# Moving most transfers of a two-block float32 network from the SyncE queue to the GpSimd queue, and its reciprocal square roots from GpSimd to VectorE

## The chip, the cores and the metric

The kernel runs on one core of a Trainium2 chip. The metric is the device time of one execution in microseconds (us). Engine names are those of the profile: PE is TensorE (PEld its weight loads), DVE is VectorE, ACT is ScalarE, POOL is GpSimd, SP is SyncE; a trailing q (SPq) means the engine's own instruction queue, where transfers are issued.

## What is computed

One sequence of 256 rows and 2048 features, float32, goes through two layers of a first block and one layer of a second. Cut to what matters here:

```
c_act = silu(c)
for l in range(2):
    mod = c_act @ w_mod[l] + b_mod[l]            # 2048 -> 3 * 2048
    shift, scale, gate = split(mod, 3)
    h = rmsnorm(x, norm_gain[l]) * (1 + scale) + shift
    proj = h @ w_in[l]                           # q_a k_a v_a g_a q_i k_i w_i q_b k_b v_b g_b
    y_a = sparse_attention(rmsnorm(q_a), rmsnorm(k_a), v_a, q_i, k_i, w_i, rel_bias) * silu(g_a)
    y_b = head_groupnorm(retention(rotary(q_b), rotary(k_b), v_b)) * silu(g_b)
    x = x + gate * (concat(y_a, y_b) @ w_out[l])
...
u = rmsnorm(x) @ w_in_2          # then a gated convolution, a gated recurrence with its own rmsnorm
x = x + (...) @ w_o_2
x = x + sigmoid(rmsnorm(x) @ w_ple_gate_2) * (p @ w_ple_proj_2)
return rmsnorm(x)
```

Every norm ends in (sum * mean + eps) ** -0.5 of a column of 1, 2 or 4 numbers per partition.

## The kernel before

**Tiles.** The 256 rows are two tiles of 128 (t = 0, 1). A weight is read in chunks of two row blocks by 512 columns (128 x 2 x 512, 512 KB). `wchunk` (L221) loads a chunk into `raw` (three buffers), ACT casts it to float32r (`whi`, L231) and DVE subtracts to get the rest (`wlo`, L233). `wgroup` (L236) then issues twelve matmuls per chunk (L249 to L251: three products, two row blocks, two row tiles).

**Modulation.** `gemv` (L333) computes the product of one row with `w_mod`, beside the matmuls and off PE: 16 transfers of 512 KB into `graw` (three buffers, L347), each followed by one DVE instruction that multiplies and accumulates (`acc`, L351 for the first, L353 for the others). One gemv of 16 gives a quarter of a layer's shift and scale (`mod_quarter`, L356, which ends in `Gm`, L366) or half of its gate (`mod_gate`, L376). There are 12 gemvs, 192 transfers. The very first one (layer 0, quarter 0, `wide`) takes six of its loads through `raw` buffers.

**Order.** Background jobs (gemvs, the bias table, selection, attention, retention) are Python generators that are stepped once per weight chunk at the rates of a table. The order that results on each engine's queue is then set by a scheduler at build time. At run time every engine works through its own list strictly in order, and so does every queue that issues transfers.

**The first ten projections of layer 0** run in four passes (`per = 4`, L834), each over a quarter of the features; a pass needs the rows scaled with that quarter's `Gm`. `bias_table` (L439) runs beside passes 1 to 3: 12 times it loads `rb` (L457), makes one-hot rows on ACT (L462 to L465), multiplies on PE (L469), copies `bt` on ACT (L471) and stores it (L472).

**The end of a layer.** `out_proj` (L874) loads the old rows (`xo`, L885), adds, stores to `xd` (L890), and at its last columns calls `drain()` (L893), which puts every background job still open ahead of what follows. Then `row_rstd` (L201: `tot`, L203, and `rstd`) gives the scale of the next layer's rows (ACT, L912).

**Issue.** SP issues all transfers but a few at the start: 512 KB weight chunks (L226), `graw` (L347), `rb`, `bt` stores, attention's `L` (L675), retention's `dec` (L756), `xo`, `xd` and the final stores. POOL issues 16 small loads at the start (L300, L308, L443).

**rstd** (L149) runs on POOL: six instructions, of which one is a power (L154). It is called 33 times.

Of the kernel before, what the change touches and what calls it, by code (L numbers as in the profile page):

```python
# [27 lines left out]
# steps of each background job per weight chunk  # L28
# [3 lines left out]
# places that instructions move forward in the order of issue  # L32
# [7 lines left out]
def shape_constants():  # L40
    """Tables that depend on shapes alone."""
# [27 lines left out]
def build(tc, a, out):  # L69
# [4 lines left out]
    with es:  # L74
# [5 lines left out]
        # ---------------------------------------------------------------- helpers  # L80
# [20 lines left out]
        def step(n=1):  # L101
            """Advance every background job by its rate."""
# [12 lines left out]
        def spawn(gen, rate, then=None):  # L115
            """Start a background job; another may follow it."""
            bg.append([gen, rate, 0.0, then])
# [10 lines left out]
        def give(consumer, t, pt):  # L128
            """Run a consumer up to its yield; what follows waits for flush()."""
            r = consumer(t, pt)  # L130
            if r is not None:
                next(r)
                late.append(r)
# [15 lines left out]
        def rstd(ss, n, mean):  # L149
            """(ss * mean + EPS) ** -0.5 for a [P, n] tile of sums of squares."""  # L150
            v = sm(n, "rv")
            G.tensor_scalar(v, ss, mean, EPS, op0=OP.mult, op1=OP.add)  # L152
            y = sm(n, "ry")
            G.tensor_tensor(y, v, mhalf[:, 0:n], op=OP.pow)  # L154
            q = sm(n, "rq")
            G.tensor_mul(q, y, y)
            G.tensor_mul(q, q, v)
            G.tensor_scalar(q, q, -0.5, 1.5, op0=OP.mult, op1=OP.add)
            z = sm(n, "rz")
            G.tensor_mul(z, y, q)  # L160
            return z
# [6 lines left out]
        def split_ps(ps, gain=None):  # L168
            """A [P, 512] transposed block in PSUM into its two float32r parts."""
# [36 lines left out]
        def build_kg(src, kg, gains, shifts):  # L206
            """One tile of four transposed blocks: normed rows scaled, shifted, split."""
# [9 lines left out]
        def build_raw(src, kg, gains):  # L217
            """Four transposed blocks of rows that are still to be normed, times the norm's gains."""
            return split_ps(transpose4(src), gains[:, kg * 4:kg * 4 + 4])

        def wchunk(srcs, n, kt):  # L221
            """Two row blocks of a weight, loaded and split."""
# [13 lines left out]
        def wgroup(srcs, n, aT, kts, consumer, mode="k", tw=3):  # L236
            """out[t] = rows[t] @ W for one group of columns; kts are row blocks (pairs from even)."""
# [41 lines left out]
        # ---------------------------------------------------------------- constants, small vectors  # L279
# [9 lines left out]
        mhalf = con.tile([P, 4], F32, name="mhalf")  # L289
        G.memset(mhalf, -0.5)  # L290
# [35 lines left out]
        # ---------------------------------------------------------------- modulation  # L326
# [6 lines left out]
        def gemv(l, ranges, wide=False):  # L333
            acc = b1.tile([P, 1024], F32, name="acc", tag="acc", bufs=2)
            for j in range(16):
# [10 lines left out]
                with tc.high_priority(offset=AHEAD["gdma"]):  # L346
                    last[1] = Y.dma_start(dst, src)  # L347
# [28 lines left out]
        def mod_gate(l, q):  # L376
            """Half q of layer l's gate, on every partition."""
            for acc in gemv(l, [4096 + 1024 * q, 4096 + 1024 * q + 512]):
                yield
            for i in range(2):  # L380
                c0 = 1024 * q + 512 * i
                gb = ev()
                Y.dma_start(gb, a["b_mod"][l, 4096 + c0:4096 + c0 + 512][None, :].to_broadcast([P, 512]))
# [10 lines left out]
        # ---------------------------------------------------------------- T5 bias table, rotary tables  # L394
# [8 lines left out]
        def rel_rotary(ap):  # L403
# [9 lines left out]
            for t in range(2):  # L413
# [4 lines left out]
                Y.dma_start(reld[t], rb[:, 0:(t + 1) * P])  # L418
# [20 lines left out]
        def bias_table(ap):  # L439
# [13 lines left out]
            for t, r0 in jobs:  # L453
# [3 lines left out]
                Y.dma_start(rb, bass.AP(tensor=reld[t].tensor, offset=reld[t].offset + r0 * ns,  # L457
                                        ap=[[32 * ns, 4], [0, 32], [1, nr * ns]]))
                h2 = nr // 2
                for hf in range(2):  # L460
# [11 lines left out]
                    Y.dma_start(bass.AP(tensor=biasd[t].tensor,  # L472
# [4 lines left out]
        # ---------------------------------------------------------------- start  # L477
# [75 lines left out]
        # ---------------------------------------------------------------- block 1  # L553
        def from_ps(pt, sb):
            """Columns in SBUF: as they are, or copied out of PSUM."""
# [6 lines left out]
        def layer(l, hT, ap):  # L562
# [62 lines left out]
            def select(t):  # L625
                """0 where a key is among the TOPK of its row and not after it, NEG elsewhere."""
# [726 lines left out]
```

## Time and profile before

| | |
|---|---|
| three runs | 1963.08, 1964.33, 1960.91 us; median 1963.08 |
| profiled execution, first to last instruction | 1964.1 us, 1.0 us above that median |
| PE busy | 1849.0 us, 94% |
| DVE busy | 1313.3 us, 67% |
| ACT busy | 1044.1 us, 53% |
| POOL busy | 93.0 us, 5% |
| moved by transfers | 440.37 MB, mean 224 GB/s |

The time of the profiled execution is its span; the page gives no other time for it, so the span is what later sums start from. The busy shares are averages over stages with different limits, so a stage is read by itself: PE's idle time in it, what the DMA engines moved in it, and which wait ended last.

### The profile page before, as it was taken

The page shows a single profiled execution, that of the slowest core. Times are in us where ns is not written, and L with a number is a line of the kernel's source. Part 1 is how long each engine was busy: PE and PEld are TensorE (multiplying, and loading weights), DVE is VectorE, ACT ScalarE, POOL GpSimd, SP SyncE. Part 2 cuts the span into 40 slices and gives each one's busy share as a digit, 9 for nine tenths or more (in the row PEclk, how much of TensorE's full clock was granted, in tenths as well). Part 3 has the DMA queues.
Part 4 walks back from the last instruction along what each step waited for, and adds up shares of the span by engine and source line. Part 5 has one row for each costly group of instructions (what it writes and reads, how often), then busy time and mean ns, then how long its engine had stood idle before and what let it go on. Part 6 is the DMA issues. An engine that isn't in the chain of part 4 may idle for free.

```text
span 1964.1 us, 24148 instructions
## 1 busy us (share of the span) xinstructions
PE 1849.0 (94%) x8670; PEld 1503.6 (77%) x8670; DVE 1313.3 (67%) x1713; ACT 1044.1 (53%) x1576; POOL 93.0 (5%) x220
## 2 busy tenths in 40 slices
PE   3988899998997999999999999999999999999997
PEld 3866577777776877688878878888888888888786
DVE  6787669998777677976755565656575545455554
ACT  3557484554435455447545675458445444445554
POOL 2000011001101002100000100000000000000100
PEclk9999899999998999999999999999999999999999
DMA  9987777987888898875547765556656666657564
GB/s 316 327 269 251 249 234 224 320 293 235 295 300 264 295 309 282 269 223 157 163 156 239 214 181 174 151 171 183 177 151 191 194 193 193 193 183 222 176 205 146
DMA packets 230921, 440.37 MB, mean 224 GB/s; under 512 B 19728, under 2 KB 32144, under 8 KB 230672
## 3 DMA queue, kind: packets, MB, share of 16 engines
q1 hardware_dynamic: 228880, 436.38, 70.5%
q10 hardware_dynamic: 1440, 2.34, 0.3%
q8 instruction: 68, 1.11, 0.2%
q14 instruction: 53, 0.43, 0.1%
q0 software_dynamic: 480, 0.10, 0.0%
HBM read 430.85 MB, written 7.91 MB: 223 GB/s over the span
## 4 chain that ended last, share of the span: by engine, by line
PE 60%; DMA 15%; DVE 11%; ACT 5%; issue 5%; POOL 3%; SPq 1%; ACTq 0%; DVEq 0%; POOLq 0%
PE mm L250 18%; PE mm L251 18%; PE mm L249 18%; DMA graw<-in_w_mod_dram 8%; DVE wlo L233 5%; DMA raw<-in_w_in_dram 4%; DMA rb<-reld 2%; ACT whi L231 2%; DVE acc L353 2%; PE tr L196 2%; PE tr L1070 1%; POOL ry L154 1%; DVE I L648 1%; POOL rv L152 1%; SPq L226 1%
## 5 line engine op out<-in xcount | busy, mean ns | idle before, releaser
L233 DVE TENSOR_TENSOR wlo<-raw,whi 128x1024 fp32r<-128x1024 f32 (+1 forms) x596 | 721.6, 1213 | 409.5 <-ACT whi L231 407.8
L231 ACT CAST whi<-raw 128x1024 fp32r<-128x1024 f32 (+1 forms) x596 | 621.9, 1045 | 696.7 <-PE mm L251 451.3
L250 PE MATMUL mm<-wlo,ah 128*128 128x512 f32 (+1 forms) x2368 | 935.8, 395 | 23.5 <-DVE wlo L233 23.2
L249 PE MATMUL mm<-whi,ah 128*128 128x512 f32 (+1 forms) x2368 | 934.5, 397 | 11.8 <-ACT ah L187 7.7
L251 PE MATMUL mm<-whi,al 128*128 128x512 f32 (+1 forms) x2368 | 931.0, 393 | 0.7 <-DVE al L188 0.6
L250 PEld LDWEIGHTS mm<-wlo,ah 128*128 128x128 f32 x2368 | 449.0, 190 | 132.2 <-DVE wlo L233 44.6
L249 PEld LDWEIGHTS mm<-whi,ah 128*128 128x128 f32 x2368 | 447.7, 189 | 108.8 <-ACT ah L187 8.4
L251 PEld LDWEIGHTS mm<-whi,al 128*128 128x128 f32 x2368 | 448.5, 189 | 92.1 <-DVE al L188 2.2
L353 DVE SCALAR_TENSOR_TENSOR acc<-graw,ct,acc 128x1024 f32<-128x1024 f32 x174 | 223.0, 1282 | 63.4 <-DMA graw<-in_w_mod_dram 62.8
L851 DVE TENSOR_TENSOR sp<-sp,mm 128x512 f32<-128x512 f32 (+1 forms) x64 | 42.0, 660 | 15.1 <-PE mm L251 15.0
L196 PE MATMUL tr<-blob,ev 128*128 128x128 f32 x192 | 34.2, 277 | 5.2 <-DVE ev L737 4.1
L179 ACT ACTIVATE ev<-tr,vT 128x128 f32<-128x128 f32 x112 | 32.4, 378 | 9.9 <-PE tr L196 9.3
L481 ACT ACTIVATE junk<-xs 128x512 bf16<-128x512 f32 (+1 forms) x42 | 25.6, 610 | 21.5 <-DMA xs<-in_x_dram 9.4
L152 POOL TENSOR_SCALAR rv<-tot 128x1 f32<-128x1 f32 (+1 forms) x9 | 3.7, 413 | 652.9 <-DVE tot L203 639.6
L154 POOL TENSOR_TENSOR ry<-rv,mhalf 128x4 f32<-128x4 f32 (+2 forms) x33 | 34.2, 1036 | 2.8
L196 PEld LDWEIGHTS tr<-blob,ev 128*128 128x128 f32 x192 | 23.6, 140 | 13.5 <-issue 6.0
L196 PE MATMUL tr<-blob,xs 128*128 128x128 f32 x128 | 24.5, 285 | 8.8 <-ACT xs L912 6.3
L462 ACT ACTIVATE oh<-rb,blob 128x512 f32<-128x512 uint8 x24 | 16.2, 715 | 27.0 <-DMA rb<-reld 27.0
L1070 PEld LDWEIGHTS tr<-X 128*128 128x128 f32 x224 | 27.0, 192 | 2.0 <-ACT uT L1119 1.0
L1070 PE MATMUL tr<-X 128*128 128x128 f32 x224 | 27.5, 276 | 0.1
L196 PEld LDWEIGHTS tr<-blob,xs 128*128 128x128 f32 x128 | 16.8, 146 | 13.8 <-ACT xs L912 7.4
L469 PE MATMUL ms<-ohr,rb 128*32 128x512 f32 x48 | 16.0, 428 | 11.2 <-ACT ohr L465 11.1
(275 smaller groups left out, 1183.8 us busy)
## 6 DMA issues: line engine op xcount, KB each, us to landing
raw<-in_w_in_dram SPq DMA_DIRECT2D x416, 512.0 KB
graw<-in_w_mod_dram SPq DMA_DIRECT2D x186, 512.0 KB
raw<-in_w_out_dram SPq DMA_DIRECT2D x64, 512.0 KB
raw<-in_w_o_dram SPq DMA_DIRECT2D x32, 512.0 KB
raw<-in_w_ple_gate_dram SPq DMA_DIRECT2D x32, 512.0 KB
raw<-in_w_a_out_dram SPq DMA_DIRECT2D x16, 512.0 KB
raw<-in_w_b_out_dram SPq DMA_DIRECT2D x16, 512.0 KB
raw<-in_w_in_dram SPq DMA_DIRECT2D x16, 256.0 KB
```

Source lines behind the costliest of these rows:

```text
L154: G.tensor_tensor(y, v, mhalf[:, 0:n], op=OP.pow)
L179: A.activation(e[:, s], ps[:, s], AF.Copy, scale=gain[:, i:i + 1])
L196: T.transpose(ps[:, s], src[:, s], ident)
L231: A.copy(hi, raw)
L233: V.tensor_sub(lo, raw, hi.bitcast(F32))
L249: T.matmul(o, ah, hi[:, j, :], start=first, stop=False)
L250: T.matmul(o, ah, lo[:, j, :], start=False, stop=False)
L251: T.matmul(o, al, hi[:, j, :], start=False, stop=end)
L353: last[0] = V.scalar_tensor_tensor(acc, rf, ct[:, j:j + 1], acc, op0=OP.mult, op1=OP.add)
L481: A.activation(junk[:, :n], src, AF.Square, accum_out=acc)
L851: V.tensor_add(h, h, pt[:, :n])
L1070: T.matmul(ps[:, h * P:(h + 1) * P], X[:, h, s], X[:, h, s], start=True, stop=True)
```

## The change

**Queues.** `gemv` loads (but for those of the first gemv), the gate's bias loads, `reld`, `rb` and bias-table stores, `L`, `dec`, `xo`, `xd` and the second block's `xo` are issued by POOL. SP keeps the weight chunks, the first gemv, the two loads of positions, and single loads and stores of the second block. **rstd** runs on DVE: an integer guess from the bits of the argument and three Newton steps, twelve dependent instructions where POOL had six.

```diff
         def rstd(ss, n, mean):
             v = sm(n, "rv")
-            G.tensor_scalar(v, ss, mean, EPS, op0=OP.mult, op1=OP.add)
+            V.tensor_scalar(v, ss, mean, EPS, op0=OP.mult, op1=OP.add)
             y = sm(n, "ry")
-            G.tensor_tensor(y, v, mhalf[:, 0:n], op=OP.pow)
-            q = sm(n, "rq")
-            G.tensor_mul(q, y, y)
-            G.tensor_mul(q, q, v)
-            G.tensor_scalar(q, q, -0.5, 1.5, op0=OP.mult, op1=OP.add)
-            z = sm(n, "rz")
-            G.tensor_mul(z, y, q)
-            return z
+            V.tensor_scalar(y.bitcast(I32), v.bitcast(I32), 1, None, op0=OP.logical_shift_right)
+            V.tensor_scalar(y.bitcast(I32), y.bitcast(I32), -1.0, 1597463007.0, op0=OP.mult, op1=OP.add)
+            for _ in range(3):
+                q = sm(n, "rq")
+                V.scalar_tensor_tensor(q, y, -0.5, y, op0=OP.mult, op1=OP.mult)
+                V.tensor_mul(q, q, v)
+                z = sm(n, "rz")
+                V.scalar_tensor_tensor(z, q, 1.5, y, op0=OP.add, op1=OP.mult)
+                y = z
+            return y
...
-                    last[1] = Y.dma_start(dst, src)
+                    last[1] = (Y if wide else G).dma_start(dst, src)
...
-                Y.dma_start(rb, bass.AP(tensor=reld[t].tensor, offset=reld[t].offset + r0 * ns,
+                G.dma_start(rb, bass.AP(tensor=reld[t].tensor, offset=reld[t].offset + r0 * ns,
...
-                    Y.dma_start(bass.AP(tensor=biasd[t].tensor,
+                    G.dma_start(bass.AP(tensor=biasd[t].tensor,
...
-                    Y.dma_start(L, biasd[t][hs].rearrange("h t s -> t h s"))
+                    G.dma_start(L, biasd[t][hs].rearrange("h t s -> t h s"))
-                    Y.dma_start(dec, a["k_dec"][:, 4 * g + h, :])
+                    G.dma_start(dec, a["k_dec"][:, 4 * g + h, :])
...
-                    Y.dma_start(xo, src[t * P:(t + 1) * P, j * 512:(j + 1) * 512])
+                    G.dma_start(xo, src[t * P:(t + 1) * P, j * 512:(j + 1) * 512])
-                    Y.dma_start(xd[t * P:(t + 1) * P, j * 512:(j + 1) * 512], n)
+                    G.dma_start(xd[t * P:(t + 1) * P, j * 512:(j + 1) * 512], n)
...
```

Comments and docstrings are dropped, so lines move by up to three. The scheduler makes a new order from the new queues. Three places show it; the names are those of the program, and `x4` is four alike in a row.

On SP, in the second pass of layer 0 (bias-table stores at L472, `rb` loads at L457), the order before was:

```order
L226 DMA raw<-in_w_in_dram 128x2x512 x2
L347 DMA graw<-in_w_mod_dram 128x2x512
L472 DMA biasd_84<-bt 4x8x512
L226 DMA raw<-in_w_in_dram 128x2x512
L472 DMA biasd_84<-bt 4x8x512
L347 DMA graw<-in_w_mod_dram 128x2x512
L457 DMA rb<-reld_86 128x1x1024
```

and over the passes of layer 0 it is now:

```order
L229 DMA raw<-in_w_in_dram 128x2x512 x3
L406 DMA pti<-in_positions_dram 128x2x1
L409 DMA tmp<-in_positions_dram 128x256
L229 DMA raw<-in_w_in_dram 128x2x512
L229 DMA raw<-in_w_in_dram 128x2x80
L229 DMA raw<-in_w_in_dram 128x2x256
L229 DMA raw<-in_w_in_dram 128x2x80
L229 DMA raw<-in_w_in_dram 128x2x256
L229 DMA raw<-in_w_in_dram 128x2x512 x18
```

Nothing stands between weight chunks on SP any more; the store that waits for `bt` stands on POOL, between `graw` loads.

On DVE, at the end of the first gemv, where the first scaled rows are made (`Sh` and `Gm` scale them, `ev` and `al` are the rows), the order before was:

```order
L353 SCALAR_TENSOR_TENSOR acc<-graw,ct,acc 128x1024 x4
L412 MEMSET hp 128x1
L441 MEMSET rbd 128x32
L314 COPY vT<-ms 128x128
L315 COPY vT_75<-ms 128x64
L363 TENSOR_TENSOR Sh_79<-tr,vT 128x4
L365 TENSOR_TENSOR mq<-tr,vT 128x4
L316 SCALAR_TENSOR_TENSOR gqk<-vT_75 128x2
L366 SCALAR_TENSOR_TENSOR Gm_77<-mq,vT 128x4
```

and is now, from that `vT` on:

```order
L315 COPY vT<-ms 128x128
L352 TENSOR_SCALAR acc<-graw,ct 128x1024
L316 COPY vT_73<-ms 128x64
L317 SCALAR_TENSOR_TENSOR gqk<-vT_73 128x2
L236 TENSOR_TENSOR wlo<-raw,whi 128x1024
L354 SCALAR_TENSOR_TENSOR acc<-graw,ct,acc 128x1024
L236 TENSOR_TENSOR wlo<-raw,whi 128x1024 x2
L354 SCALAR_TENSOR_TENSOR acc<-graw,ct,acc 128x1024
L411 CAST posf<-pti 128x2
L364 TENSOR_TENSOR Sh_77<-tr,vT 128x4
```

After that `Sh` come two more `acc`, with `mq` between them, and only then `Gm`: five `acc` of the second gemv and three `wlo` have moved ahead of the first `Gm`.

On DVE, at the end of layer 0 (`tot` is the sum of squares of the new rows, `rv` to `rz` are rstd), the order now is:

```order
L206 TENSOR_REDUCE tot<-ssx 128x1
L236 TENSOR_TENSOR wlo<-raw,whi 128x1024
L153 TENSOR_SCALAR rv<-tot 128x1
L888 TENSOR_TENSOR xs<-mm,gate 128x512
L155 TENSOR_SCALAR ry<-rv 128x1
L354 SCALAR_TENSOR_TENSOR acc<-graw,ct,acc 128x1024
L156 TENSOR_SCALAR ry<-ry 128x1
L354 SCALAR_TENSOR_TENSOR acc<-graw,ct,acc 128x1024
L159 SCALAR_TENSOR_TENSOR rq<-ry 128x1
L354 SCALAR_TENSOR_TENSOR acc<-graw,ct,acc 128x1024
L160 TENSOR_TENSOR rq<-rq,rv 128x1
```

Two more `acc` stand between the later steps of that rstd; before, rstd stood on POOL and DVE had other work after `tot`.

How many `wlo` (weight chunks split) and `acc` (gemv loads used) stand ahead of some points in DVE's list, counted in both orders:

| point in DVE's order | before: wlo, acc | now: wlo, acc |
|---|---|---|
| `Gm` of layer 0, quarter 0 | 0, 16 | 3, 21 |
| quarter 1 | 19, 32 | 20, 42 |
| quarter 2 | 39, 48 | 40, 59 |
| quarter 3 | 58, 64 | 60, 77 |
| `Gm` of layer 1, quarter 0 | 129, 118 | 130, 129 |
| `tot` of layer 0, row tile 0 | 153, 130 | 154, 155 |
| `tot` of layer 0, row tile 1 | 155, 133 | 155, 160 |
| `Gm` of layer 1, quarter 3 | 194, 163 | 194, 177 |
| end | 596, 192 | 596, 192 |

## Rows read from the trace of the kernel before

**Rows 1.** The page: busy shares, and PE and DMA in 40 equal slices

```profile
PE 1849.0 (94%) x8670; PEld 1503.6 (77%) x8670; DVE 1313.3 (67%) x1713; ACT 1044.1 (53%) x1576; POOL 93.0 (5%) x220
PE   3988899998997999999999999999999999999997
DMA  9987777987888898875547765556656666657564
```

**Rows 2.** Stretches: us, busy us (instructions) per engine, PEclk, DMA share, GB/s

```profile
40.00:95.00 55.00, 51.67 (x234) 43.07 (x235) 43.64 (x47) 31.15 (x43) 0.00 (x0) 0.94 0.95 324
95.00:167.00 72.00, 62.42 (x271) 46.09 (x270) 57.52 (x80) 40.36 (x63) 2.53 (x2) 1.00 0.83 266
167.00:248.00 81.00, 67.68 (x278) 50.26 (x277) 54.73 (x61) 49.86 (x76) 0.00 (x0) 0.92 0.77 246
248.00:395.00 147.00, 140.59 (x652) 108.51 (x650) 124.67 (x213) 92.89 (x176) 14.13 (x36) 0.98 0.81 263
395.00:514.00 119.00, 110.67 (x577) 89.79 (x576) 106.25 (x165) 60.56 (x111) 11.68 (x24) 0.99 0.82 270
514.00:603.00 89.00, 78.88 (x339) 62.99 (x338) 59.97 (x65) 39.06 (x56) 3.74 (x6) 0.95 0.87 288
603.00:723.00 120.00, 113.55 (x526) 93.36 (x526) 84.32 (x81) 60.73 (x84) 2.50 (x6) 0.98 0.88 292
723.00:850.00 127.00, 118.24 (x569) 92.90 (x569) 109.47 (x182) 61.00 (x112) 16.21 (x36) 1.00 0.84 277
```

**Rows 3.** The same view, the stretch that moved most

```profile
60.00:80.00 20.00, 20.00 (x89) 16.30 (x88) 15.38 (x13) 11.26 (x15) 0.00 (x0) 1.00 1.00 357
```

**Rows 4.** One line's instructions: duration min/median/max, first to last start

```profile
L366 DVE SCALAR_TENSOR_TENSOR Gm<-mq,vT x8: 155/158/165, 39.8 to 722.9; 128x4 f32<-128x4 f32 x8
```

**Rows 5.** Waits, whole run: total us, times, longest

```profile
SPq L347 <- DVE acc L353: 58.4, 49, 3.8
SPq L472 <- ACT bt L471: 54.3, 15, 7.9
DVE nm L780 <- POOL rz L160: 13.2, 8, 2.3
```

**Rows 6.** The chain of waits, 90 to 250 us, by line

```profile
by line: DMA rb<-reld 22.8%; DMA graw<-in_w_mod_dram 10.8%; DMA raw<-in_w_in_dram 8.7%; issue 7.3%; DVE wlo L233 5.3%; ACT whi L231 5.1%; PE mm L250 4.7%; ACT oh L462 3.9%; PE mm L251 3.9%; PE mm L249 3.7%; ACT oh L463 3.6%; DVE acc L353 3.
```

**Rows 7.** Costliest groups: count, busy us, mean ns, idle before

```profile
L233 DVE TENSOR_TENSOR wlo<-raw,whi 128x1024 fp32r<-128x1024 f32 (+1 forms) x596 | 721.6, 1213 | 409.5 <-ACT whi L231 407.8
L353 DVE SCALAR_TENSOR_TENSOR acc<-graw,ct,acc 128x1024 f32<-128x1024 f32 x174 | 223.0, 1282 | 63.4 <-DMA graw<-in_w_mod_dram 62.8
```

**Rows 8.** The timeline at the start: start us, us

```profile
43.33 0.79 PE L249 MATMUL mm<-whi,ah 128*128 128x512 f32 x1 [3.86 <-ACT ah L187]
```

**Rows 9.** The timeline at the end of layer 0

```profile
589.90 0.15 DVE L203 TENSOR_REDUCE tot<-ssx 128x1 f32<-128x4 f32 x1
594.33 1.95 ACT L912 ACTIVATE xs<-xs,rz 128x512 f32<-128x512 f32 x3 [2.90 <-POOL rz L160]
```

**Rows 10.** DVE's timeline, two dependent small instructions

```profile
1102.56 0.17 DVE L955 TENSOR_TENSOR lb<-lb,lb 128x8 f32<-128x8 f32 x1
1102.76 0.17 DVE L956 TENSOR_TENSOR lb<-lb 128x8 f32<-128x8 f32 x1
```

**Rows 11.** ACT in the last stretch of the timeline

```profile
1952.34 0.72 ACT L1287 ACTIVATE xs<-xs,rz 128x512 f32<-128x512 f32 x1 [2.23 <-POOL rz L160]
```

**Rows 12.** Transfers issued by POOL at the start, and DVE beside them

```profile
4.96 0.62 POOL L308 DMA_DIRECT2D ev<-in_conv_w_dram  x1
9.01 0.50 POOL L308 DMA_DIRECT2D ev<-in_q_norm_gain_dram  x1 [1.70 <-DMA ev<-in_b_mod_dram]
4.68 0.80 DVE L351 TENSOR_SCALAR acc<-graw,ct 128x1024 f32<-128x1024 f32 x1 [3.70 <-DMA graw<-in_w_mod_dram]
7.97 1.28 DVE L353 SCALAR_TENSOR_TENSOR acc<-raw,ct,acc 128x1024 f32<-128x1024 f32 x1 [2.49 <-DMA raw<-in_w_mod_dram]
```

**Rows 13.** Groups of POOL's instructions: count, busy us, mean ns, idle before

```profile
L300 POOL DMA_DIRECT2D ev<-in_b_mod_dram x2 | 1.0, 506 | 0.0
```

More of the change, by code (lines that the diff above doesn't have):

```diff
@@ L287, in build @@
         lev = con.tile([P, 7, P], U8, name="lev")
-        mhalf = con.tile([P, 4], F32, name="mhalf")
-        G.memset(mhalf, -0.5)
         vT = con.tile([P, 128], F32, name="vT")
@@ L382, in mod_gate @@
                 gb = ev()
-                Y.dma_start(gb, a["b_mod"][l, 4096 + c0:4096 + c0 + 512][None, :].to_broadcast([P, 512]))
+                G.dma_start(gb, a["b_mod"][l, 4096 + c0:4096 + c0 + 512][None, :].to_broadcast([P, 512]))
                 pm = trt()
@@ L417, in rel_rotary @@
                 V.tensor_scalar(rb, rel, 0.0, 128.0, op0=OP.max, op1=OP.min)
-                Y.dma_start(reld[t], rb[:, 0:(t + 1) * P])
+                G.dma_start(reld[t], rb[:, 0:(t + 1) * P])
             yield
@@ L1253, in f @@
                     xo = ev()
-                    Y.dma_start(xo, xd[t * P:(t + 1) * P, j * 512:(j + 1) * 512])
+                    G.dma_start(xo, xd[t * P:(t + 1) * P, j * 512:(j + 1) * 512])
                     n = xs()
```

## The prediction, written before the change was run

> **What bounds the kernel now.** I read the page first [rows 1]: PE is busy 94% of the span. By slices it is at nine tenths in nearly all of the second half, where DMA is at 5 to 7 tenths; what PE loses lies in the first 850 us, where DMA stands at 7 to 9. So only that part can change much, and I cut it at the starts of `Gm` [rows 4] and read each stretch [rows 2]. PE idles for 55.00 - 51.67 = 3.3 us before 95 us, 9.6 and 13.3 in the next two (the bias-table passes), 6.4 and 8.3 in the middle of layer 0, 10.1 up to 603 us, 6.5 and 8.8 in layer 1. The sum is 66.3 us, which is all that a better flow of transfers could give there.
>
> Next, why. The transfer rate says which stretches are full: 324 GB/s at a DMA share of 0.95 before 95 us, but 266 and 246 in the bias-table passes. The fastest stretch that I found moved 357 at a share of 1.00 [rows 3]. So up to 95 us the kernel is near the rate of its transfers, while from 95 to 248 us it is held by waits: SP stood 54.3 us in all before bias-table stores whose `bt` was not ready, and 58.4 us before gemv loads whose buffer DVE still held [rows 5]; all transfers behind them waited too. The chain of waits agrees: from 90 to 250 us, 22.8% of it is `rb` landing, 10.8% gemv loads and 8.7% weights [rows 6].
>
> **The change part by part.** One load is 128 x 1024 x 4 bytes, 0.524 MB. The counts of `wlo` and `acc` are those of the table of the two orders; each `acc` needs one gemv load and each `wlo` one weight chunk, and DVE takes them strictly in that order, so a load that has moved ahead of a point must have landed before that point.
>
> *Up to the second `Gm`.* Ten more gemv loads must land before it (42 for 32). That is 5.24 MB, at 324 GB/s 16.2 us; at 357 it would be 14.7. DVE has room for them: it was busy 43.6 of 55 us, and ten times 1.28 us [rows 7] fits into the longer stretch. PE's first weight matmul was at 43.33 us [rows 8], and it now stands behind five `acc` whose loads are only issued as buffers come free, so PE starts some 10 us later; this lies inside the 16.2 and is not added. I take +16.2.
>
> *Bias-table passes, 95 to 248 us.* `rb` loads and `bt` stores leave SP, so weight chunks flow past them. Four loads more than before must land (20 to 60 and 42 to 77, for 19 to 58 and 32 to 64): 39.1 MB + 2.1 = 41.2, at 324 GB/s 127 us, under PE's own 130.1. So the gain is at most PE's idle time, 22.9 us, and at least 0, because the waits go to POOL with the stores, and the gemv loads behind them are then late for DVE. Of the transfers on the chain `rb` is 22.8 of 42.3, or 54%, and it is `rb` and `bt` that no longer hold weights; I take that share, -12.3.
>
> *Middle of layer 0, 248 to 514 us.* The loads are nearly as many as before (70 `wlo` and 52 `acc` for 71 and 54). Ten rstds fall here. Each is twelve dependent instructions at 0.20 us from start to start and 0.17 us of busy time [rows 10]: 10 x 12 x 0.17 = 20.4 us of DVE, against which stand waits for POOL's `rz` such as the 13.2 us over eight calls [rows 5]. DVE idles 22.3 and 12.8 us in the two stretches, so most is covered; if nothing were, it would be +13. I take +3.
>
> *End of layer 0, 514 to 603 us.* Between the `Gm` and the second `tot` there were 26 `wlo` and 15 `acc`; now 25 and 31. The stretch moved 288 x 89 us = 25.6 MB; with 15 loads more it is 33.5 MB, which at 324 GB/s takes 103.4 us: +14.4. At 357 it would be +4.9.
>
> *The rstd at that point.* Before, 4.4 us passed from `tot` to ACT's use [rows 9]. Now the twelve steps take 12 x 0.20 = 2.4 us, but five `acc` (6.4 us) and a `wlo` and an add (1.9) stand in the list between them: 10.7 us, so +6.3 at most, and nothing if the other row tile, which is ready later, sets PE's start. I take half, +3.2.
>
> *Layer 1, 603 to 850 us.* Here the lead is paid back: 32 `acc` remain, for 59. PE idles 15.2 us there, which bounds the gain. 27 of 59 loads are gone; I take that share of it, -7.0.
>
> *The rest.* From 850 us on PE is saturated but for a few us, and what moves there is hidden behind it. At the very end there are two rstds in a row before the last stores; ACT waited 2.23 us for the first [rows 11], where twelve steps at 0.20 make about 2.4 and the last step's hand-over is about as before; with both, +0.8, between 0 and 2.
>
> *Issuing on POOL.* This is 176 gemv loads and some 115 others. POOL was busy 93 us. Its small transfers of 24 and 2 rows took 0.62 and 0.50 us to issue [rows 12]. A gemv load has 256 rows of 2 KB; no row shows its price. From below it is 0.50 us, and from above, if it went by rows, 256 / 32 x 0.51 = 4.1 us, with the 0.51 of the two 32-row loads of the modulation's bias [rows 13]. Between 2 and 24 rows the price rose by 0.12 us, so I take it near the lower end, 0.5 to 1 us, at which POOL hides it: DVE uses a load every 2.3 us at most.
>
> That POOL's 0.62 us transfer ended 0.10 us after a DVE tensor_scalar that ran from 4.68 to 5.48 us, while one issued inside a scalar_tensor_tensor kept to 0.50 [rows 12]. The Trainium skill (SBUF — State Buffer, The "DVE blocks DMA" trap) says that a transfer issued from GpSimd cannot have its descriptors written while DVE runs an instruction in a mode that takes both ports, and advises against issuing there. The two rows agree with it as far as one pair can. By it only the first `acc` of each gemv would hold POOL, twelve times 0.75 us, so 9 us spread over 850, behind three buffers: the sum stays. Without the rule, if any DVE instruction held POOL, each load would be late by up to 1.28 us, which three buffers cover at one load per 2.3 us or more.
>
> **Sum.** 16.2 - 12.3 + 3 + 14.4 + 3.2 - 7.0 + 0.8 = +18.3, and 1964.1 + 18.3 = 1982.4 for the profiled execution; it stands 1.0 above the median, so the forecast is 1981. With each term at its bounds, the forecast's own range is 1967 to 1998. A measurement of this kernel tells about 0.2%, 3.9 us, from no change.
>
> **The rivals.**
>
> *1, faster: weights no longer wait, and the lead costs little.* If SP's free queue takes all of PE's idle time in the bias-table passes (-22.9) and in layer 1 (-15.2), and transfers in two queues reach 357 GB/s where one reached 324, the first stretch costs (17.8 + 5.24) / 0.357 - 55 = +9.6 and the end of layer 0 +4.9; with the tail's 0.8 it is -22.8, so 1940. For it speaks that SP's waits were long [rows 5]; against it that the first stretch was already at a DMA share of 0.95 [rows 2]. The Trainium skill (DMA: Bandwidth & Descriptors, Issuing engines are not separate DMA queues) says that transfers from all issuers run on the same engines and gain only issue time. By that rule the two terms stay at +16.2 and +14.4; no row here shows two busy queues in a steady stretch.
>
> *2, slower still: POOL becomes the bound.* If a 256-row load costs 4.1 us to issue, 26 loads before the second `Gm` take 107 us instead of 71 (+36), and 31 at the end of layer 0 take 127 instead of 103 (+24): 2041. It decides from 71 / 26 = 2.7 us per issue. Against it speaks the small rise with rows.
>
> *3, no change.* If the bias-table passes give their full 22.9 us and the lead costs what I forecast, the sum is +18.3 - 10.6 = +7.7; with layer 1's full 15.2 it is -0.5, so 1963. It needs all of PE's idle time to come from transfers, though some of it is ACT's own order.
>
> **How the numbers follow.** Forecast 0.46, rival 1 0.28, rival 3 0.16, rival 2 0.10. Faster by over 0.2% is rival 1 and a third of rival 3: 0.33. Within 0.2% is most of the rest of rival 3 and the low edge of the forecast: 0.12. Slower is the rest, 0.55. The range runs from just under rival 1's time to above the forecast's own range, 1938 to 2005; outside lie the further half of rival 1's spread, about 0.1, and rival 2.
>
> **What would show it.** The second `Gm` should start near 111 us instead of 95, with the DMA share near 0.95 throughout, and PE's first weight matmul near 53 us. From there to the fourth `Gm` it should take about 141 us, not 153. The two `tot` of layer 0 should come some 25 us later than before, in a stretch at 320 GB/s or more, and layer 1 should then lose less of PE than 15 us. POOL's busy time should rise by 150 to 300 us, with each gemv load at 0.5 to 1 us. I am wrong in the main step if the second `Gm` comes no later than 100 us; wrong on POOL's price if a load takes over 2.7 us there; and wrong on the bias-table passes if PE still idles over 20 us in them.

## The result and the profile after

| | before | after |
|---|---|---|
| median of the runs taken together, us | 1962.24 (1960.91 to 1964.33, 4 runs) | 1997.11 (1993.12 to 2002.84, 4 runs) |
| span of the profiled execution, us | 1964.1 | 1996.3 |
| ratio of times | 1 | 1.0179, 95% interval 1.0161 to 1.0198 |

The change makes the kernel slower by 1.8%, 35 us by the ratio and 32.2 us between the two profiled executions. The forecast was 1981 us, between 1938 and 2005, slower with a chance of 0.55: the side is right and the time lies in the range, but the loss is almost twice the forecast's 18.

The page of the changed kernel first: busy shares, PE and its granted clock in 40 slices, and the two queues of transfers (packets, MB, share of 16 engines).

```profile
PE 1856.0 (93%) x8670; PEld 1516.8 (76%) x8670; DVE 1356.9 (68%) x2109; ACT 1044.0 (52%) x1576; POOL 194.3 (10%) x311
...
PE   2789999998885999999999999999999999999997
...
PEclk9999999999797999999999999999999999999999
...
q1 hardware_dynamic: 172960, 322.02, 52.4%
q0 software_dynamic: 35360, 114.49, 17.0%
```

PE's busy time rose only 7 us over [rows 1], so the rest is idle time, and the slices show where: PE is under nine tenths in the first three (150 us) and from 450 to 650 us, where its granted clock falls too. A quarter of the bytes now goes through POOL's queue (q0).

To see which stretch lost what, I take marks that both kernels pass: the start of the 20th, 59th, 129th and 241st `wlo` (weight chunks, which come in the same order) and the two `tot` at the end of layer 0. A stretch's loss is the change in its length.

| mark (us) | before | after | later by | the stretch lost | forecast for it |
|---|---|---|---|---|---|
| 20th `wlo` | 95.0 | 119.0 | 24.0 | +24.0 | +16.2 |
| 59th `wlo` | 248.2 | 254.1 | 5.9 | -18.1 | -12.3 |
| 129th `wlo` | 511.5 | 515.9 | 4.4 | -1.5 | +3 |
| first `tot` | 589.9 | 619.2 | 29.3 | +24.9 | +14.4 |
| second `tot` | 602.9 | 639.4 | 36.5 | +7.2 | +3.2 |
| 241st `wlo` | 870.7 | 900.4 | 29.7 | -6.8 | -7.0 |
| end | 1964.1 | 1996.3 | 32.2 | +2.5 | +0.8 |
| sum | | | | +32.2 | +18.3 |

Every large term has the sign that was forecast. (The forecast set its +14.4 up to the second `tot`; the table puts it at the first, ahead of which the loads must land, and the +3.2 for rstd between the two.) The same stretches of the changed kernel, as the view of stretches has them (columns as in [rows 2]):

```profile
41.90:119.00 77.10, 58.27 (x251) 46.22 (x251) 56.09 (x73) 42.30 (x66) 28.36 (x40) 0.89 0.92 303
119.00:254.10 135.10, 120.03 (x516) 94.27 (x515) 110.16 (x125) 85.90 (x127) 36.83 (x56) 0.95 0.90 295
254.10:515.90 261.80, 243.39 (x1219) 193.87 (x1217) 233.02 (x482) 140.25 (x256) 48.36 (x75) 1.00 0.78 258
515.90:619.20 103.30, 90.78 (x351) 71.55 (x351) 75.97 (x87) 37.87 (x59) 31.84 (x48) 0.87 0.91 319
619.20:639.40 20.20, 6.61 (x19) 5.24 (x20) 11.73 (x25) 7.62 (x17) 4.09 (x7) 0.58 0.71 254
639.40:900.40 261.00, 251.04 (x1185) 205.70 (x1184) 188.26 (x334) 131.33 (x204) 15.47 (x30) 0.99 0.71 224
```

Set against [rows 2], the first one moves 303 GB/s where 324 was seen, for 77 us instead of 55; PE idles 18.8 us in it, for 3.3. The second, where PE idled 22.9 us, now has 15.1 in a shorter stretch. From 515.9 us to the first `tot` PE idles 12.5 us and the transfers move 319 GB/s. Between the two `tot` PE is busy for a third of 20 us.

The four `Gm` of layer 0 and the first weight matmul (timeline: start us, us, engine, line, operation) answer to [rows 8] and to the times 39.8, 94.9, 167.3 and 248.1 behind [rows 4]:

```profile
52.12 0.16 DVE L367 SCALAR_TENSOR_TENSOR Gm<-mq,vT 128x4 f32<-128x4 f32 x1
...
121.78 0.15 DVE L367 SCALAR_TENSOR_TENSOR Gm<-mq,vT 128x4 f32<-128x4 f32 x1
...
192.88 0.16 DVE L367 SCALAR_TENSOR_TENSOR Gm<-mq,vT 128x4 f32<-128x4 f32 x1
...
258.87 0.16 DVE L367 SCALAR_TENSOR_TENSOR Gm<-mq,vT 128x4 f32<-128x4 f32 x1
```

```profile
54.72 0.80 PE L252 MATMUL mm<-whi,ah 128*128 128x512 f32 x1 [11.91 <-ACT ah L190]
```

PE starts its weights 11.4 us later. From the second `Gm` to the fourth it takes 137.1 us (forecast 141, before 153.2).

Last, the layer boundary, DVE and ACT in the timeline:

```profile
619.25 0.15 DVE L206 TENSOR_REDUCE tot<-ssx 128x1 f32<-128x4 f32 x1
...
626.51 0.16 DVE L160 TENSOR_TENSOR rq<-rq,rv 128x1 f32<-128x1 f32 x1
628.52 1.29 DVE L354 SCALAR_TENSOR_TENSOR acc<-graw,ct,acc 128x1024 f32<-128x1024 f32 x1 [1.85 <-DMA graw<-in_w_mod_dram]
629.73 0.15 DVE L162 SCALAR_TENSOR_TENSOR rz<-rq,rz 128x1 f32<-128x1 f32 x1
...
639.40 0.16 DVE L206 TENSOR_REDUCE tot<-ssx 128x1 f32<-128x4 f32 x1 [0.79 <-ACT junk L482]
```

```profile
629.91 2.56 ACT L913 ACTIVATE xs<-xs,rz 128x512 f32<-128x512 f32 x4 [10.29 <-DVE rz L162]
```

The twelve steps of `rstd` begin after `tot` at 619.25; the last but one is done at 626.7, but the last stands in DVE's list behind an `acc` that waits 1.85 us for its gemv load. ACT gets its scale 10.7 us after `tot`, where it was 4.4 [rows 9]. Four `acc` stand ahead of the last step, not five: where the section on the change has two more between the later steps, the timeline has one, at 628.52, and the next behind the last step.

### The profile page after: what moved, and what is told of

It reads as the page before. It is cut to its first block, busy times and chain, and to the rows that moved or that the text cites. A ratio compares the mean times of both kernels' runs of the same rounds, so it can differ in the third digit from the quotient of the medians.

```text
span 1996.3 us, 24510 instructions
## 1 busy us (share of the span) xinstructions
PE 1856.0 (93%) x8670; PEld 1516.8 (76%) x8670; DVE 1356.9 (68%) x2109; ACT 1044.0 (52%) x1576; POOL 194.3 (10%) x311
## 3 DMA queue, kind: packets, MB, share of 16 engines
q8 instruction: 68, 1.11, 0.2%
## 4 chain that ended last, share of the span: by engine, by line
PE 51%; issue 10%; DMA 7%; DVE 4%; ACT 2%; POOL 0%; ACTq 0%; SPq 0%; DVEq 0%; POOLq 0%
PE mm L252 15%; PE mm L253 15%; PE mm L254 15%; DMA graw<-in_w_mod_dram 3%; DVE wlo L236 2%; PE tr L1071 1%; DMA raw<-in_w_out_dram 1%; DMA raw<-in_w_in_dram 1%; PE tr L199 1%; ACT whi L234 1%; DVE acc L354 1%; DMA dec<-in_k_dec_dram 1%; PE tr L362 0%; DMA lev_i<-in_k_lev_dram 0%; PE ms L638 0%
## 5 line engine op out<-in xcount | busy, mean ns | idle before, releaser
L348 POOL DMA_DIRECT2D graw<-in_w_mod_dram x176 | 115.2, 655 | 478.7 <-DVE acc L354 297.6
L1255 POOL DMA_DIRECT2D ev<-xd x8 | 4.3, 541 | 725.2 <-PE tr L199 400.0
L676 POOL DMA_DIRECT2D L<-biasd x12 | 8.8, 733 | 184.1 <-PE tr L699 168.8
L649 DVE SCALAR_TENSOR_TENSOR I<-sc,wi,I 128x128 f32<-128x128 f32 (+1 forms) x60 | 24.9, 414 | 0.7 <-ACT sc L642 0.2
```

The source lines that it names most:

```text
L348: last[1] = (Y if wide else G).dma_start(dst, src)
```

## The experiments

Times of runs are compared as ratios to the kernel before on the same chip. Theory A is the prediction's: what costs is the lead of the gemv loads. Theory B: it is rstd on DVE. Theory C: it is the issue by POOL, or the second queue, by itself.

**One part at a time**

*rstd alone.* In the kernel before, only the body of `rstd` is the new one:

```diff
-            G.tensor_scalar(v, ss, mean, EPS, op0=OP.mult, op1=OP.add)
+            V.tensor_scalar(v, ss, mean, EPS, op0=OP.mult, op1=OP.add)
...
```

> Only the reciprocal square roots move to DVE; all transfers stay where they were. Theory A (the gemv loads' own queue lets them run ahead, and they take transfer time from the weights): no change up to 500 us, the second Gm at 95 +- 3 us, and only the boundary between the layers loses a few us by acc instructions standing inside the twelve steps: 1963 to 1972. Theory B (the twelve steps on DVE are what costs, at the boundary and in layer 0): most of the change's 35 us appears here, 1980 or more.

Measured: ratio 1.0056 (1.0037 to 1.0075), 11 us. The 20th `wlo` is at 95.3 us, the 129th 7.4 us earlier than before, and the loss is made at the boundary: the 161st `wlo` is 16.6 us late. DVE and ACT in the timeline there:

```profile
592.82 0.15 DVE L205 TENSOR_REDUCE tot<-ssx 128x1 f32<-128x4 f32 x1
...
597.73 1.28 DVE L353 SCALAR_TENSOR_TENSOR acc<-graw,ct,acc 128x1024 f32<-128x1024 f32 x1
...
599.04 1.28 DVE L353 SCALAR_TENSOR_TENSOR acc<-graw,ct,acc 128x1024 f32<-128x1024 f32 x1
...
601.59 0.16 DVE L161 SCALAR_TENSOR_TENSOR rz<-rq,rz 128x1 f32<-128x1 f32 x1
```

```profile
601.79 2.56 ACT L912 ACTIVATE xs<-xs,rz 128x512 f32<-128x512 f32 x4 [5.96 <-DVE rz L161]
```

From `tot` to ACT's use it takes 9.0 us, for 4.4 on POOL. Two `acc` and two `wlo` stand between the steps. The median, 1975.9 us, lies between the ranges of the two theories: B falls as the main cause, but A had the boundary's price too small.

*Queues alone.* All transfers move, `rstd` stays on POOL (the diff of the change without its first part).

> Only the queues move; rstd stays on POOL. Here 45 gemv loads stand ahead of the second Gm, for 32 before and 42 in the full change. Theory A: the second Gm at 120 to 128 us and the whole at 1985 to 2000. Theory B: under 1980. Besides, POOL's rstd now stands in one list with gemv loads that wait for buffers: if that matters, the step from tot to the scaled rows at the layer boundary grows beyond the 4.4 us of before.

Measured: 1.0283 (1.0242 to 1.0324), 56 us: worse than the whole change. The second `Gm` is at 122.8 us as theory A had it, but the time, 2021.5 us, lies above its range. The next kernel has the same wait for POOL's rstd with fewer parts moved.

*gemv loads alone.*

```diff
-                    last[1] = Y.dma_start(dst, src)
+                    last[1] = (Y if wide else G).dma_start(dst, src)
```

> Only the gemv loads move to POOL; bias table, L, dec, xo, xd stay on SP and rstd on POOL. Theory A: the lead (46 loads ahead of the second Gm) is all here, so 1985 to 2000, with the second Gm at 120 to 128 us. Theory C (any transfer issued by POOL costs, by itself or by contention): only the part that belongs to these loads, and the next kernel is slower than before too.

Measured: 1.0168 (1.0127 to 1.0209), 33 us; the second `Gm` is at 126.2 us, as theory A had it, and the 20th `wlo` 27.4 us late. This one line makes a loss of the size of the whole change's. The wait of ACT at the layer boundary for POOL's rstd (total us, times, longest), in the kernel before and in this one:

```profile
ACT xs L912 <- POOL rz L160: 6.1, 2, 3.2
```

```profile
ACT xs L912 <- POOL rz L160: 18.6, 2, 13.8
```

Issues that wait for a buffer and the small steps of rstd now share one list in order, so rstd waits with them.

*All but the gemv loads*, rstd on POOL (the diff of the change without that line and without rstd).

> All queue moves but the gemv loads, which stay on SP; rstd stays on POOL. The order keeps 32 gemv loads ahead of the second Gm and 48 and 64 ahead of the next two. Theory A: the second Gm at 95 +- 3, the bias-table passes shorter by 5 to 15 us since stores no longer hold weights on SP, at the layer boundary 11 loads more than before are ahead of the first tot (+3 to +8): 1945 to 1962. Theory C: slower than 1968.

Measured: 1.0004 (0.9983 to 1.0026). The second `Gm` stays at 96.8 us and the 59th `wlo` comes 26.0 us earlier, more than the 5 to 15 of theory A. But 24 of these are lost again by the end, and the median, 1966.4 us, lies between the two ranges.

*Without xo and xd too*: gate bias, bias table, `L` and `dec` on POOL.

> Only bias-table loads and stores, L, dec and the gate's bias move to POOL; gemv loads, xo and xd stay on SP, rstd on POOL. In the kernel with xo and xd moved too, 26 us were won by the 59th wlo and 24 of them lost again by the end, with POOL's rstd standing behind xd stores and xo loads at both layer ends. If that is the loss: 1943 to 1955. If the loss is the gemv lead at the end of layer 0 (137 acc ahead of the first tot here, 144 there, 130 before): half of it remains, 1952 to 1960.

Measured: 0.9906 (0.9882 to 0.9931), 18 us faster than before. SP's waits between the 20th and the 59th `wlo`, in the kernel before:

```profile
SPq L472 <- ACT bt L471: 45.1, 10, 7.9
SPq L226 <- DVE wlo L233: 16.8, 11, 3.6
```

and in this one, and its stretch from the 20th to the 59th `wlo`:

```profile
SPq L226 <- DVE wlo L233: 47.7, 26, 4.1
SPq L347 <- DVE acc L353: 11.8, 9, 2.7
```

```profile
96.20:224.90 128.70, 120.80 (x522) 93.10 (x521) 109.75 (x136) 95.43 (x147) 20.79 (x32) 0.97 0.94 304
```

Before, SP stood 45.1 us before stores whose `bt` was not ready, with weights behind them, and only 16.8 before full weight buffers. Now it is held mostly by full weight buffers (47.7), which is as it should be; transfers ran at 304 GB/s and PE idled 7.9 us, for 22.9. The 59th `wlo` is 23.3 us earlier than before, and the end of the profiled execution still 21.2. That this is because POOL's list holds no xd store ahead of rstd is a reading; a later kernel bears out part of it.

*The bias table alone.*

```diff
-                Y.dma_start(reld[t], rb[:, 0:(t + 1) * P])
+                G.dma_start(reld[t], rb[:, 0:(t + 1) * P])
...
-                Y.dma_start(rb, bass.AP(tensor=reld[t].tensor, offset=reld[t].offset + r0 * ns,
+                G.dma_start(rb, bass.AP(tensor=reld[t].tensor, offset=reld[t].offset + r0 * ns,
...
-                    Y.dma_start(bass.AP(tensor=biasd[t].tensor,
+                    G.dma_start(bass.AP(tensor=biasd[t].tensor,
```

> Only the bias table's loads and stores (reld, rb, bt) move to POOL. Theory: these are what held the weights on SP in the bias-table passes, so the 59th wlo comes 20 to 26 us earlier than before, as with L, dec and the gate's bias moved too, and the whole is within 5 us of that kernel's 1946. If L and dec on SP hold weights as much later on, 1950 to 1958.

Measured: 0.9902 (0.9878 to 0.9926), 19 us faster; the 59th `wlo` 23.3 us earlier. These three issues are all of the gain, and this kernel and the last one are faster than both kernels of the case.

*The change with the gemv loads back on SP.*

> All moves but the gemv loads, and rstd on DVE, so the changed kernel with gemv loads back on SP. With rstd on POOL this gave 1966, and without xo and xd on POOL 1946. If POOL's list (rstd behind xd stores that wait for their rows, xo loads behind them) makes these 20 us, rstd on DVE takes them away: 1946 to 1956. If it is the gemv lead at the end of layer 0 (144 acc ahead of the first tot here too, 137 in the faster one), or xo behind xd: 1962 to 1975.

Measured: 0.9941 (0.9911 to 0.9971), 12 us faster than before. So with xd and xo on POOL, rstd on DVE is better by 12 us than rstd on POOL (1.0004), which is 12 of the 20 us that xd and xo had cost; in the kernel before, with all transfers on SP, it was worse by 11. And it is the gemv loads that turn 0.9941 into 1.0179: they cost about 47 us.

**What of the gemv loads costs**

*xo and xd back on SP, in the changed kernel.*

> The changed kernel with xo and xd back on SP; the order on DVE is that of the changed kernel. Its second tot came 20.1 us after the first, for 13.0 before, because an xo load stood behind five gemv loads on POOL. If that is so, the two tot are 13 to 15 us apart here and the whole is 4 to 8 us shorter than the changed kernel, 1989 to 1993. If the distance comes from DVE's own list (acc between the steps), no change.

Measured: 1.0152 (1.0124 to 1.0181), not clearly apart from the change's 1.0179, and the two `tot` are 18.2 us apart (changed 20.2, before 13.0). So the `xo` load makes 2 us of that distance at most, and the first of the two expectations missed; the DVE timeline shows why:

```profile
623.90 0.15 DVE L205 TENSOR_REDUCE tot<-ssx 128x1 f32<-128x4 f32 x1
...
633.52 1.28 DVE L353 SCALAR_TENSOR_TENSOR acc<-graw,ct,acc 128x1024 f32<-128x1024 f32 x1 [2.54 <-DMA graw<-in_w_mod_dram]
634.72 0.15 DVE L161 SCALAR_TENSOR_TENSOR rz<-rq,rz 128x1 f32<-128x1 f32 x1
...
642.07 0.16 DVE L205 TENSOR_REDUCE tot<-ssx 128x1 f32<-128x4 f32 x1
```

The same `acc` stands ahead of the last step, and waits 2.54 us for its load; the second `tot` follows from that. So the distance comes from DVE's own list, as with rstd alone, whose two `tot` are 18.0 us apart.

*The lead on SP's queue.*

```diff
-RATE = {"rows": 0.902,
+RATE = {"rows": 1.3,
```

> The kernel before, all transfers on SP and rstd on POOL, with one number changed: the rate of the first gemvs, 1.3 for 0.902, so that about 41 acc stand ahead of the 20th wlo, as in the changed kernel (before 32). Theory A: the 20th wlo at 112 to 120 us (before 95.0), with no transfer on POOL. Theory C: under 105 us. What is won later by the early Gm is open: 1955 to 1985 in all.

Measured: 1.0041 (1.0023 to 1.0059). With 37 `acc` ahead of the 20th `wlo` (not 41), it came at 107.2 us: five loads more cost 12.2 us, without POOL. So a lead costs by itself, which is theory A's part (its 112 to 120 us were for 41); C's bound of 105 is passed. That is 2.4 us a load, more than the 1.6 that one load takes at 324 GB/s; why was not tried.

*The lead taken away, POOL still issuing.* One edge at build time puts each `acc` behind the latest `wlo` of the program:

```diff
-                V.tensor_sub(lo, raw, hi.bitcast(F32))
+                lw[0] = V.tensor_sub(lo, raw, hi.bitcast(F32))
...
-                with tc.high_priority(offset=AHEAD["gdve"]):
+                with tc.high_priority(offset=AHEAD["gdve"]), (tc.issue_after(lw[0].ins) if lw[0] else nullcontext()):
```

> The whole change, but each gemv instruction on DVE is ordered behind the wlo that stands ahead of it in the program, so that 33, 48, 64 acc stand ahead of the second, third and fourth Gm (before 32, 48, 64; changed 42, 59, 77) and 122 to 129 ahead of the two tot (before 130, 133; changed 155, 160). POOL still issues every gemv load, and DVE still makes rstd. Theory A (the lead costs, not POOL): the 20th wlo at 95 to 100 us instead of 119, the 59th 15 to 25 us earlier than before, as in the kernel with all moves but the gemv loads, and 1945 to 1968 in all. Theory C (loads issued by POOL cost by themselves): 1985 or more, as with the changed kernel.

Measured: 1.0125 (1.0091 to 1.0158). The 20th `wlo` is at 107.3 us with as many `acc` ahead as before (32), above A's 95 to 100; the 59th is 11.9 earlier than before, for A's 15 to 25. The median, 1988.7 us, lies in theory C's range, but this edge also holds 29 `acc` back until after the 241st `wlo`, so the total says less than the marks.

*The same by another edge*: each `acc` behind the previous `Gm`.

```diff
-            V.scalar_tensor_tensor(Gm[l][:, s], t, 1.0, norm_g[l][:, s], op0=OP.add, op1=OP.mult)
+            gm[0] = V.scalar_tensor_tensor(Gm[l][:, s], t, 1.0, norm_g[l][:, s], op0=OP.add, op1=OP.mult)
...
-                with tc.high_priority(offset=AHEAD["gdve"]):
+                with tc.high_priority(offset=AHEAD["gdve"]), (tc.issue_after(gm[0].ins) if gm[0] else nullcontext()):
```

> The whole change, with one edge more: each gemv's DVE instructions are ordered behind the Gm of the gemv before it. That alone leaves 16, 32, 48, 64 acc ahead of the four Gm of layer 0, as before, and 130 and 140 ahead of the two tot (before 130, 133). The held kernel lost 12 us up to the 20th wlo with no extra load, since the first Gm stood behind four acc of the next gemv and three wlo on DVE. If that is the cause: first weight matmul at 43 to 46 us, the 20th wlo at 95 to 99, the 59th 18 to 26 us earlier than before. The boundary of the layers still loses about 10 us by acc between the twelve steps: 1950 to 1970. If loads issued by POOL cost by themselves (theory C): the 20th wlo at 105 or later, and 1980 or more.

Measured: 1.0089 (1.0068 to 1.0109). The lead is gone (32, 64 and 130 `acc` ahead of the 20th and 59th `wlo` and of the first `tot`), and so is most of the loss at the end of layer 0: the first `tot` is at 589.5 us, before 589.9, and the stretch from the 129th `wlo` to it takes 83.2 us, for 103.3 in the changed kernel and 78.4 before. The 20th `wlo` is still 16.0 us late and the median 1983.9 us, both as theory C had it, and the boundary loses another 20 us up to the 161st. Issues from 45 to 111 us (count, KB each, median us to landing) here, and in the kernel with the gemv loads on SP:

```profile
graw<-in_w_mod_dram POOLq DMA_DIRECT2D x16, 512.0 KB, 6.9
raw<-in_w_in_dram SPq DMA_DIRECT2D x16, 512.0 KB, 6.3
rb<-reld POOLq DMA_DIRECT2D x6, 128.0 KB, 7.5
```

```profile
graw<-in_w_mod_dram SPq DMA_DIRECT2D x18, 512.0 KB, 4.8
raw<-in_w_in_dram SPq DMA_DIRECT2D x18, 512.0 KB, 4.1
```

A weight chunk lands in 6.3 us here, in 4.1 there. And six `rb` loads come in this stretch, for none: with SP's queue freed the bias table also began early.

*The early table taken away as well*: its one-hot rows on ACT behind the latest `whi`.

```diff
-                A.copy(hi, raw)
+                lh[0] = A.copy(hi, raw)
...
-                    A.activation(oh, rb[:, hf * h2:(hf + 1) * h2, :].rearrange("p a b -> p (a b)"), AF.Abs, bias=bmid)
+                    with tc.issue_after(lh[0].ins):
+                        A.activation(oh, rb[:, hf * h2:(hf + 1) * h2, :].rearrange("p a b -> p (a b)"), AF.Abs, bias=bmid)
```

> The kernel with acc behind the earlier Gm, and one edge more: the one-hot rows of the bias table on ACT stay behind the whi cast that precedes them in the program, so that 24 casts stand ahead of the first of them, not 8. With acc alone put back, the 20th wlo still came at 111.0 us (before 95.0), with six rb loads in the queue of POOL and seven one-hot groups on ACT before it, which the kernel before had none of. If that early table is the rest of the loss: the 20th wlo at 96 to 101 us. If it is the gemv loads in a queue of their own beside the weights (a weight chunk landed in 6.3 us there, in 4.1 with both in SP's queue): 105 or later. In all 1970 to 1985 in the first case, if nothing is given back, 1980 to 1990 in the second.

Measured: 1.0110 (1.0071 to 1.0150); the 20th `wlo` at 107.5 us. Waits of ACT's casts for weights from 45 to 111 us, here and with the gemv loads on SP:

```profile
ACT whi L235 <- DMA raw<-in_w_in_dram: 19.5, 9, 4.2
```

```profile
ACT whi L233 <- DMA raw<-in_w_in_dram: 4.2, 3, 1.7
```

So, by one profile of each kernel, the early table is 3.5 of the 16 us, and 12.5 remain that go with the gemv loads on POOL: weights land late. The transfers are not full meanwhile. This kernel up to its 20th `wlo`:

```profile
40.00:107.50 67.50, 54.90 (x239) 43.73 (x238) 47.33 (x68) 30.75 (x50) 16.06 (x24) 0.90 0.87 285
```

These are 19.2 MB at a share of 0.87, for 17.8 MB at 0.95 in the kernel before [rows 2]. The 1.4 MB more are worth 4 us at 324 GB/s; the other 8 are a lower rate, and by the lower share most of that is waiting, not transfers in each other's way. PE's start may be part of it (first weight matmul at 51.2 us, for 46.4 with these loads on SP); how it divides was not tried. Nor did any kernel issue the gemv loads from a third engine, so a queue of their own and the issue by POOL are not told apart.

## Why the prediction came out as it did

The side was right, and so was the sign of each large term; the first stretch and the end of layer 0 were sized too small. That the time lies in the forecast's own range, 1967 to 1998, says little: the bounds that its terms name give about 1945 to 2015.

**The first stretch (+16.2, measured +24.0): right in kind, near in size partly by luck.** The step that failed is the assumption that ten loads more are the whole cost. With the lead taken away 16.0 us were still lost up to the 20th `wlo`: 12.5 go with the gemv loads on POOL and 3.5 with the early table, both put at nothing. The lead itself makes the other 8, half of its 16.2.

The step "this lies inside the 16.2 and is not added", on PE's later start, is in doubt too. Three stretches of the changed kernel:

```profile
55.00:85.00 30.00, 27.40 (x117) 22.16 (x118) 20.13 (x23) 12.55 (x19) 10.86 (x17) 0.93 0.78 249
85.00:120.00 35.00, 30.68 (x130) 23.51 (x128) 26.38 (x35) 26.62 (x42) 11.75 (x17) 0.95 1.01 343
573.20:619.60 46.40, 39.11 (x157) 29.72 (x155) 38.02 (x37) 16.45 (x20) 13.16 (x19) 0.96 0.97 349
```

From 55 to 85 us, just after that start, DMA's share was 0.78, where it stood near 1 before [rows 3]: weight buffers were full while PE had only begun (SP waited up to 12.9 us at a time for a `wlo` to free one), and the lost transfer time did not come back. But its price is not shown. No kernel moved PE's start alone, and in two that began their weights 3 us late (rstd alone at 47.0 us, gemv loads back on SP at 46.4) the 20th `wlo` came at 95.3 and 95.2 us, as before.

**Bias-table passes (-12.3, measured -18.1): right, but too small.** The cause is shown by the kernel that moves the table alone: 23 to 26 us are to be had. That is more than PE's idle time of 22.9, which the forecast took as the most, in part since fewer matmuls fall between these marks (522 in the kernel that moves tables, `L` and `dec`, 548 before). The changed kernel, with 76 `acc` ahead of the 59th `wlo` for 64, kept 18.1.

**Middle of layer 0 (+3, measured -1.5).** rstd alone made the 129th `wlo` 7.4 us earlier: I had counted steps on DVE as a cost, and the waits for POOL that go as cover alone. That these waits are the gain is argued, not tested apart. Nor did it last: in that kernel the first `tot` is 2.9 us late, with 16 `acc` between the two marks for 12.

**End of layer 0 (+14.4, measured +24.9).** The step had 33.5 MB in 103.4 us at 324 GB/s, and 33.0 MB in 103.3 us, at 319 GB/s, is what was measured. The term was mis-sized by where it ends: I set the stretch to the second `tot`, 89 us, but the loads have to land before the first, and the 13 us between the two cannot take them. That the two sums agree is chance: 31 loads were set in the longer stretch, and 28 lie in the shorter, which held 12 before. That the lead is the cause is shown: without it, the first `tot` came at 589.5 us. And over the fourteen kernels here this stretch takes 78 to 81 us with 12 or 14 `acc` in it, 83 to 89 with 16 to 19, 96 with 21 (gemv loads on SP) and 101 to 103 with 28. That is about 1.5 us a load, whichever engine issues it, so 16 more make the 24.9.

**The boundary (+3.2, measured +7.2).** I took half of the upper bound of 6.3, and all of it came: ACT's use was 10.7 us after `tot`, as worked out in that bound (10.7), though by luck, with four `acc` and a wait of 1.85 us where five `acc` were counted. That "the other row tile sets PE's start" was no excuse; both tiles were late.

**Layer 1 (-7.0, measured -6.8) and the tail.** Right. The +2.5 behind the 241st `wlo` is made up to the first `tot` of layer 1's end, which is 32.2 us late; from the last `tot` to the end it is 0.4.

**Issue on POOL: right.** The loads' issue on POOL (count: min, median, max in ns, first to last start):

```profile
L348 POOL DMA_DIRECT2D graw<-in_w_mod_dram x176: 530/711/1113, 33.8 to 790.3; - x176
```

0.53 us for gate loads and 0.71 for those of two column pieces, far from 4.1: rival 2 is out. POOL's issues took 184 us more, but its busy time rose by 101, below the 150 to 300 named, because I had left out that rstd's own 82 us go. The bound on a DVE instruction was seen once in the steady part: an issue that ran through a whole tensor_scalar `acc`,

```profile
141.71 1.11 POOL L348 DMA_DIRECT2D graw<-in_w_mod_dram  x1 [3.27 <-DVE acc L354]
142.98 0.71 POOL L348 DMA_DIRECT2D graw<-in_w_mod_dram  x1 [0.16 <-issue]
```

```profile
141.93 0.75 DVE L352 TENSOR_SCALAR acc<-graw,ct 128x1024 f32<-128x1024 f32 x1
```

It took 1.11 us and ended 0.14 after that `acc`. This agrees with the rule (the Trainium skill, SBUF — State Buffer, The "DVE blocks DMA" trap), and with the pair in [rows 12]; it is worth 0.4 us here, where the prediction had left room for 9 behind the buffers. Of the seven issues that overlap a tensor_scalar `acc`, this one, which began 0.22 us ahead of it, and the three that began inside it all end 0.11 to 0.22 us after it. The three that began 0.34 to 0.47 us ahead end within it, at their usual length.

**Rival 1** named its two conditions. The weights' part came true (23 to 26 us). The rate of 357 did not come where it would have paid: the first stretch moved 303 GB/s and the end of layer 0 319. It came in one slice of 50 us, inside the end of layer 0:

```profile
549.00:599.00 50.00, 43.40 (x178) 33.65 (x176) 38.49 (x37) 17.59 (x23) 14.09 (x21) 0.97 0.99 358
```

With both queues in use that is 358 GB/s at a share of 0.99, and one queue had 357 at 1.00 [rows 3]: when the engines are full, two queues move no more than one. This agrees with the Trainium skill (DMA: Bandwidth & Descriptors, Issuing engines are not separate DMA queues). **Rival 3** fails with the first stretch.

## What to carry to other kernels

A transfer that waits in a queue holds all that stands behind it, so moving late stores off the weights' queue paid (1% from three lines). Moving the bulk loads of a background job did not: in the weights' queue they had been paced by it, in a queue of their own they ran ahead and took transfer time from what PE needed next, and held back from that they still cost 12 us in the first stretch. Before moving a load, ask what paced it, and count at each due point how many now stand ahead; and keep small dependent steps out of a list, POOL's or DVE's, in which something waits for a transfer.

## What was not expected of the hardware

PE's granted clock. Mean over the span, before and after:

```profile
core 0: 1964.1 us, clock 0.986
```

```profile
core 0: 1996.3 us, clock 0.976
```

It fell from 0.986 to 0.976, and PE's busy time for the same 8670 matmuls rose by 7.0 us. The stretches show where: 0.89 behind PE's late start, 0.87 and 0.58 around the layer boundary, each after PE had idled (before, 0.94 in the first and 0.95 up to the second `tot` [rows 2]). Around the first weight matmul:

```profile
46.00:58.00 12.00, 3.29 (x8) 2.57 (x9) 8.82 (x16) 2.78 (x6) 4.14 (x6) 0.50 0.81 273
```

That matmul took 0.80 us, after 11.9 us of idle time, at 0.50 of full speed, the lower level of 1.2 GHz; the page's mean for its line is 398 ns. The kernel before began no faster (0.79 us [rows 8]), so this start is only later, not dearer. What the added waits can cost a second time, in the matmuls behind them, is at most these 7 us, and no term of the prediction held it.
